# A third seven-product pair for the keys and values of a cross-attention

## The chip, the cores and the metric

The kernel runs on one core of a Trainium2 chip. The metric is the time of one execution on the device in microseconds (us), the median of three runs. Engines are called by the profile's names: PE is TensorE's matmul, PEld its weight load, DVE VectorE, ACT ScalarE, POOL GpSimd, SP the engine that issues the loads.

## What is computed

One encoder layer on x (256 frames x 2048) with 256 memory tokens, all float32: a half-step SwiGLU, a mixer of pooling and gated linear attention, cross-attention on the memory, a second half-step SwiGLU, a last norm. The change touches the keys and values of the cross-attention alone:

```python
def mem_cross_attention(h, mem_h, w_q, w_kv, w_o):
    q = (h @ w_q).reshape(b, s, XATTN_HEADS, XATTN_HEAD_DIM)             # 4 heads of 512
    kv = (mem_h @ w_kv).reshape(b, mem_h.shape[1], 2, XATTN_HEADS, XATTN_HEAD_DIM)
    k, v = kv[:, :, 0], kv[:, :, 1]
    logits = jnp.einsum('bshd,bmhd->bhsm', q, k).astype(jnp.float32) * (XATTN_HEAD_DIM ** -0.5)
    p = jax.nn.softmax(logits, axis=-1).astype(v.dtype)
    o = jnp.einsum('bhsm,bmhd->bshd', p, v).reshape(b, s, D_MODEL)
    return o @ w_o
```

So `mem_h @ w_kv` is a product of 256 x 2048 by 2048 x 4096.

## The kernel before

**Float32 as two halves.** Each float32 operand is split into a high part (a rounded copy, made by ScalarE) and a low part (the rest, a subtraction on VectorE), and a product of two operands is three matmuls: high by high, high by low, low by high. Activations lie transposed in `xs` and `ys`, by 16 k-tiles of 128, high and low; the 256 rows are two halves of 128. A weight tile `raw` is split into `wh` and `wl`.

**Blocks and units.** `block_s` computes 1024 output columns (two groups of 512, j = 0 and 1). It walks over the 2048 inner elements in eight units, each a pair g of k-tiles: one transfer of 1 MB from the weights, a split, then products on TensorE. Keys and values take four blocks, in this order: first key block (heads 0 and 1), first value block, second key block, second value block.

**Plain units.** In a plain unit (`unit_p`) each of 2 banks x 2 halves x 2 k-tiles takes 3 matmuls of 128 x 512: 24. Its split is one `wh` (ScalarE, 128 x 2048, line 1579) and one `wl` (VectorE, line 453).

**Sevens.** A pair with its 2 k-tiles, 2 halves and 2 groups of columns is a 2 x 2 by 2 x 2 product of blocks, and can be had with seven block products in place of eight, from sums of blocks. Such a unit (`unit_s`, `seven`) takes 7 x 3 = 21 matmuls (line 507). Its split (`split_seven`) makes four sums of weight blocks, T (three VectorE additions, line 486), splits three blocks of `raw` themselves into `xh` and `xl` (lines 279, 280; products P1, P3 and P2 read them) and T into `wh` and `wl` (lines 489, 453; P5, P7, P6 and P4 read them). Sums of activation blocks are made once for each pair by `Sums.make` (lines 424 to 436 on VectorE, then two splits, lines 285 and 286); they lie in a tile `ye`, and one of them takes the place of a part of `xs`, so that a pair whose sums are made is a seven from then on. `Sums("ye", xs, (0, 4), True, 2)` names the pairs 0 and 4, and room for two in one tile. The parts of the first seven of a block open two further bank pairs; after the last seven `combine` adds the parts (lines 574 to 579), and after the last unit `join` adds them to the whole (line 589).

**Buffers.** `raw`, `wh` and `wl` have three buffers each. T, `xh` and `xl` have homes that change with the stage. In the feed-forward stages each tag has its own; during keys and values these hold, so that `xh` and `xl` both come from the two buffers called "att":

```python
    KV_HOMES = {"T": [("sg", D, 2)], "xh": [("att", 3 * NB, 2)], "xl": [("att", 3 * NB, 2)]}
```

**Order.** `Stream` emits units in sequence, with the splits two units ahead of the products. `st.op(f, n)` puts other work n units later: `turn_K` transposes and splits keys, `logits` and `probs` make the softmax, `values` multiplies with it, `mem_fold` turns the memory into `xs`. `among_weights` and `in_turn` keep VectorE's and ScalarE's work in the order of emission among the splits; beyond that a planner of the framework sets the order of each engine's instructions when the kernel is built, and on the chip each engine runs its own in that order. Part of a `wl` next to a `combine` or `join` goes to GpSimd (line 457). Loads are issued by SP, one for each unit, when a `raw` buffer is free.

The eight pairs of a block come in the order `KV_ORDER = (1, 5, 2, 0, 3, 6, 4, 7)` in all four blocks: pair 0 is a seven in fourth place, pair 4 in seventh. The sums of pair 0 are made at the start of the first key block, those of pair 4 after its second unit.

Of the kernel before, what the change touches and what calls it, by code (L numbers as in the profile page):

```python
# [20 lines left out]
NB = 512  # L21
# [78 lines left out]
def build(ctx, tc, I, out):  # L100
# [89 lines left out]
    xs = main.tile([P, KT, 2, S], F32R, tag="xs", name="xs")  # L190
# [79 lines left out]
    def among_weights(f):  # L270


        scalar, vector = behind_weights(f)
        latest["vector"] = vector
        if scalar is not None:
            latest["scalar"] = scalar
# [349 lines left out]
    def wload(dst, w, k0, n, n0, cols=NB):  # L626
        nc.sync.dma_start(
            dst, w[k0 * P : (k0 + n) * P, n0 : n0 + cols].rearrange("(k p) n -> p k n", p=P)
        )
# [9 lines left out]
    def wwide(w, n0, k0=0, nk=KT):  # L639

        def src(k):
            def load(raw):
                raw = raw.rearrange("p (k n) -> p k n", n=2 * NB)
                if len(loaded) < 3:
                    for kk in range(2):
                        parts = (0, NB) if not loaded else (0,)
                        for c in parts:
                            n = 2 * NB // len(parts)
                            wload(raw[:, kk : kk + 1, c : c + n], w, k + kk, 1, n0 + c, n)
                else:  # L650
                    wload(raw, w, k, 2, n0, 2 * NB)
                next(first_loads, None)
                loaded.append(1)
            return load
        return [src(k0 + k) for k in range(0, nk, 2)]
# [577 lines left out]
    def homes(of):  # L1233
        return lambda: scope.update(shared={tag: list(of[tag]) for tag in of})
# [47 lines left out]
    w_q, w_kv, w_o = I["xattn_w_q"][0], I["xattn_w_kv"][0], I["xattn_w_o"][0]  # L1282
# [2 lines left out]
    q_sums, Q_ORDER = Sums("ye", xs, (4, 5), True, 2), ((0, 1, 2, 3, 6, 4, 5, 7),  # L1285
                                                        (0, 1, 4, 2, 5, 3, 6, 7))
    Q_SEVENS = ((4,), (4, 5))
    kv_sums, KV_ORDER = Sums("ye", xs, (0, 4), True, 2), (1, 5, 2, 0, 3, 6, 4, 7)
    held = {}

    def ev_Q(b):
# [10 lines left out]
    def turn_K(h):  # L1302
        v = rows_turned(held["K", h])
        K = xa["K", h] = xt("K", [P, 4, 2, M], F32R, tag="kv", bufs=2)
        split(K[:, :, 0, :], K[:, :, 1, :], v)

    def ev_V(b):
        def evict(j, c):
            V = xa["V", 2 * b + j] = xt("V", [P, 2, 2, XHD], F32R, tag="kv", bufs=2)
            split(V[:, :, 0, :], V[:, :, 1, :], c)  # L1310
        return evict

    def logits(h):
        ps = ptile(uid("pl"))
        for t in range(2):
            tok = slice(t * P, (t + 1) * P)
            parts = [(d, a, b) for d in range(4) for a, b in ((0, 0), (0, 1), (1, 0))]
            for i, (d, a, b) in enumerate(parts):
                nc.tensor.matmul(  # L1319
                    ps[:, t, :M], ys[:, 4 * h + d, a, tok], xa["K", h][:, d, b, :],  # L1320
                    start=i == 0, stop=i == 11,
                )
        scale = XHD ** -0.5
        nm, sm = xt("nm", [P, 2], bufs=2), xt("sm", [P, 2], bufs=2)
        nc.vector.tensor_reduce(out=nm, in_=ps[:, :, :M], axis=AX.X, op=ALU.max)
        nc.vector.tensor_scalar_mul(nm, nm, -scale)
        pr = xa["P", h] = xt("P", [P, 2, M], bufs=2)
        for t in range(2):
            nc.scalar.activation(
                pr[:, t, :], ps[:, t, :M], AF.Exp, scale=scale, bias=nm[:, t : t + 1],  # L1330
                accum_out=sm[:, t : t + 1],
            )
        nc.vector.reciprocal(out=sm, in_=sm)
        for t in range(2):
            nc.vector.tensor_scalar_mul(pr[:, t, :], pr[:, t, :], sm[:, t : t + 1])

    def probs(h):
        ps = ptile(uid("pt"))
        for mtile in range(2):
            for t in range(2):  # L1340
                nc.tensor.transpose(
                    ps[:, mtile, t * P : (t + 1) * P], xa["P", h][:, t, mtile * P : (mtile + 1) * P], ident
                )
        if h % 2 == 0:
            xt("PT", [P, D], F32R)
        PT = xa["PT", h] = xa["PT"][:, h % 2 * 4 * S : (h % 2 + 1) * 4 * S].rearrange(
            "p (m a s) -> p m a s", m=2, a=2
        )
        split(PT[:, :, 0, :], PT[:, :, 1, :], ps[:, :, :S])

    def values(h):
        for p in range(2):
            ps = ptile(uid("pv"))
            for d in range(2):
                col = slice((2 * p + d) * P, (2 * p + d + 1) * P)
                parts = [(m, a, b) for m in range(2) for a, b in ((0, 0), (0, 1), (1, 0))]
                for i, (m, a, b) in enumerate(parts):
                    nc.tensor.matmul(  # L1358
                        ps[:, d, :S], xa["V", h][:, m, a, col], xa["PT", h][:, m, b, :],
                        start=i == 0, stop=i == 5,  # L1360
                    )
            split_pair(ys, 4 * h + 2 * p, ps[:, :, :S])
# [8 lines left out]
            for c, after in enumerate((5, 7, 6, 9)):  # L1371
                st.op(lambda c=c: mem_fold(c), after)
    st.op(homes(KV_HOMES))
    for g, after in zip(kv_sums.pairs, (0, 2)):
        st.op(lambda g=g: among_weights(lambda: kv_sums.make(g)), after)
    for b in range(2):
        block_s(wwide(w_kv, b * 2 * NB), xs, kv_sums, KV_ORDER, lambda j, c, b=b: held.__setitem__(
            ("K", 2 * b + j), c))
        for j in (1, 0):
            h = 2 * b + j  # L1380
            st.op(lambda h=h: turn_K(h), 1)
        for h in (2 * b, 2 * b + 1):
            st.op(lambda h=h: logits(h), 2)
            st.op(lambda h=h: probs(h), 3)
        block_s(wwide(w_kv, D + b * 2 * NB), xs, kv_sums, KV_ORDER, ev_V(b))
        for h in (2 * b, 2 * b + 1):
            st.op(lambda h=h: values(h), 1)
# [211 lines left out]
def program(shapes):  # L1599
    import concourse.bacc as _bacc  # L1600

    nc = _bacc.Bacc("TRN2", target_bir_lowering=False, num_devices=1)
    args = {
        name: nc.dram_tensor(f"in_{name}", shapes[name], F32, kind="ExternalInput").ap()
        for name in _INS
    }
    out = nc.dram_tensor("out", _OUT, F32, kind="ExternalOutput").ap()
    with tile.TileContext(nc, schedule_with_timeline_sim=True) as tc, ExitStack() as ctx:
        build(ctx, tc, args, out)
    return nc  # L1610
# [10 lines left out]
```

## Time and profile before

| | |
|---|---|
| median of three runs | 2083.23 us (2082.67 to 2083.72) |
| the profiled execution | 2082.87 us |
| its span, first to last instruction | 2081.1 us |
| mean granted TensorE clock | 0.999 |
| PE busy | 2069.6 us (99%) |
| DVE busy | 1786.6 us (86%) |
| ACT busy | 1138.7 us (55%) |
| DMA, mean | 209 GB/s |

Times in the profile are those of one execution. A busy time of PE counts pipelined matmuls with modelled ends, so the pace of TensorE is read from starts: a run of n matmuls in the chain and its length. The name of a tile tells its kind: L507 products are those of sevens, L362 those of plain units. In a row of groups the last column is the idle time of the engine just before such instructions and what ended it. The four blocks of keys and values lie between 1090 and 1290 us.

### The profile page before, as it was taken

What the parts mean: (1) busy time and instruction counts of PE and PEld (TensorE: products, weight loads), DVE (VectorE), ACT (ScalarE), POOL (GpSimd) and SP (SyncE); (2) the same over time, 40 slices, a digit from 0 to 9 for tenths busy, and PEclk for the clock granted to TensorE, in tenths of its full rate; (3) what the DMA queues carried; (4) which work ended last, traced back from release to release, by engine and by line L of the source; (5) the groups of instructions that cost most, each with busy time, mean ns of one, the idle gap of its engine ahead of it and who ended that gap; (6) DMA issues with size and microseconds to landing.
All of it is one profiled execution on the core that took longest, in us unless ns stands there. A gap on an engine that the chain in (4) does not pass through costs nothing.

```text
span 2081.1 us, 24343 instructions
## 1 busy us (share of the span) xinstructions
PE 2069.6 (99%) x9660; PEld 1727.6 (83%) x9660; DVE 1786.6 (86%) x1670; ACT 1138.7 (55%) x1128; POOL 98.4 (5%) x87
## 2 busy tenths in 40 slices
PE   9999999999999999999999999999999999999998
PEld 7888888888888888888888888888888888888886
DVE  7998899989998677679788777879988999889987
ACT  7655455644654545455755444656554555545554
POOL 0000000000000000000000000000100010000001
PEclk9999999999999999999999999999999999999999
DMA  7666666566656755557655455666576665676664
GB/s 264 207 201 227 235 223 219 185 223 239 227 199 218 249 167 182 162 185 272 226 179 190 162 182 180 205 222 203 181 242 212 237 207 193 223 242 222 210 226 151
DMA packets 131178, 435.95 MB, mean 209 GB/s; under 512 B 9844, under 2 KB 13528, under 8 KB 130680
## 3 DMA queue, kind: packets, MB, share of 16 engines
q1 hardware_dynamic: 130888, 433.86, 61.9%
q8 instruction: 76, 1.25, 0.2%
q10 hardware_dynamic: 176, 0.53, 0.1%
q14 instruction: 38, 0.31, 0.0%
HBM read 417.58 MB, written 16.78 MB: 209 GB/s over the span
## 4 chain that ended last, share of the span: by engine, by line
PE 99%; DMA 0%; DVE 0%; ACT 0%; SPq 0%; DVEq 0%; issue 0%; ACTq 0%
PE pt L362 59%; PE pt L507 27%; PE pa L347 7%; PE pb L362 2%; PE ph L780 1%; PE pl L1319 1%; PE pv L1358 1%; PE px L791 1%; PE pp L1012 0%; PE pe L362 0%; DMA x<-in_x 0%; PE pa L1039 0%; PE po L1161 0%; PE tm L1267 0%; PE px L717 0%; PE pq L1148 0%
## 5 line engine op out<-in xcount | busy, mean ns | idle before, releaser
L362 PE MATMUL pt<-wh,xs 128*128 128x512 f32 x2128 | 682.4, 390 | 0.1
L453 DVE TENSOR_TENSOR wl<-raw,wh 128x2048 fp32r<-128x2048 f32 (+1 forms) x256 | 552.1, 2162 | 141.7 <-ACT wh L1579 141.3
L1579 ACT CAST wh<-raw 128x2048 fp32r<-128x2048 f32 x256 | 489.4, 1913 | 300.7 <-PE pt L362 134.5
L362 PEld LDWEIGHTS pt<-wh,xs 128*128 128x128 f32 x2128 | 398.7, 188 | 81.9 <-ACT xs L236 0.4
L362 PE MATMUL pt<-wh,ys 128*128 128x512 f32 x1472 | 463.9, 389 | 0.0
L489 ACT CAST wh<-T 128x1024 fp32r<-128x1024 f32 x236 | 248.1, 1055 | 366.7 <-DVE T L486 355.8
L362 PE MATMUL pt<-wl,xs 128*128 128x512 f32 x1064 | 414.5, 390 | 0.0
L362 PEld LDWEIGHTS pt<-wh,ys 128*128 128x128 f32 x1472 | 276.2, 188 | 56.9
L362 PE MATMUL pt<-wl,ys 128*128 128x512 f32 x736 | 286.8, 390 | 0.0
L453 DVE TENSOR_TENSOR wl<-T,wh 128x2048 fp32r<-128x2048 f32 (+1 forms) x118 | 264.7, 2243 | 0.8 <-ACT wh L489 0.4
L362 PEld LDWEIGHTS pt<-wl,xs 128*128 128x128 f32 x1064 | 199.8, 188 | 41.0
L280 DVE TENSOR_TENSOR xl<-raw,xh 128x1536 fp32r<-128x1536 f32 x118 | 206.7, 1751 | 18.9 <-ACT xh L279 18.9
L279 ACT CAST xh<-raw 128x1536 fp32r<-128x1536 f32 x118 | 174.6, 1480 | 44.0 <-PE pt L507 35.1
L486 DVE TENSOR_TENSOR T<-T,raw 128x512 f32<-128x512 f32 x236 | 162.9, 690 | 6.2
L362 PEld LDWEIGHTS pt<-wl,ys 128*128 128x128 f32 x736 | 138.2, 188 | 28.6
L486 DVE TENSOR_TENSOR T<-raw 128x1024 f32<-128x1024 f32 x118 | 143.8, 1218 | 0.5
L507 PE MATMUL pt<-wh,xs 128*128 128x512 f32 x364 | 141.8, 390 | 0.0
L457 POOL TENSOR_TENSOR wl<-raw,wh 128x768 fp32r<-128x768 f32 x40 | 74.1, 1852 | 1376.2 <-DVE wl L453 1339.2
L507 PE MATMUL pt<-xh,xs 128*128 128x512 f32 x364 | 135.8, 389 | 0.0
L347 PE MATMUL pa<-xs,wh 128*128 128x512 f32 x384 | 135.6, 397 | 0.0
L507 PE MATMUL pt<-wh,xe 128*128 128x512 f32 x320 | 124.3, 389 | 0.0
L347 PE MATMUL pa<-xs,wl 128*128 128x256 f32 x384 | 106.8, 282 | 0.0
(248 smaller groups left out, 2312.4 us busy)
## 6 DMA issues: line engine op xcount, KB each, us to landing
raw<-in_ffn_w_down SPq DMA_DIRECT2D x88, 1024.0 KB, 5.6
raw<-in_ffn_w_up SPq DMA_DIRECT2D x80, 1024.0 KB, 5.0
raw<-in_ffn_w_gate SPq DMA_DIRECT2D x77, 1024.0 KB, 5.1
raw<-in_w_in SPq DMA_DIRECT2D x32, 1024.0 KB, 5.3
raw<-in_xattn_w_kv SPq DMA_DIRECT2D x32, 1024.0 KB, 5.0
raw<-in_w_out SPq DMA_DIRECT2D x16, 1024.0 KB, 5.6
raw<-in_xattn_w_q SPq DMA_DIRECT2D x16, 1024.0 KB, 5.6
raw<-in_xattn_w_o SPq DMA_DIRECT2D x16, 1024.0 KB, 5.6
```

What stands on the lines that cost most here:

```text
L279: in_turn("scalar", lambda: nc.scalar.copy(hi, src))
L280: in_turn("vector", lambda: nc.vector.tensor_tensor(out=lo, in0=src, in1=f32(hi), op=ALU.subtract))
L347: nc.tensor.matmul(o, w, x, start=k == 0 and i == 0, stop=last and i == 1)
L362: nc.tensor.matmul(ps, a, w, start=first and i == 0, stop=last and i == 2)
L453: in_turn("vector", lambda: nc.vector.tensor_tensor(out=lo[:, :n], in0=src[:, :n], in1=f32(hi[:, :n]), op=ALU.subtract))
L457: rest = nc.gpsimd.tensor_tensor(out=lo[:, n:], in0=src[:, n:], in1=f32(hi[:, n:]), op=ALU.subtract)
L486: in_turn("vector", lambda: nc.vector.tensor_tensor(out=o, in0=a, in1=b, op=ALU.add))
L489: in_turn("scalar", lambda: nc.scalar.copy(th[:, c], t[:, c]))
L507: nc.tensor.matmul(banks[n], x, w, start=n in fresh and j == 0, stop=n in ends and j == 2)
L780: nc.tensor.transpose(v[:, i, h * P : (h + 1) * P], g[:, h, i * P : (i + 1) * P], ident)
L791: nc.tensor.transpose(v[:, j, h * P : (h + 1) * P], x[:, h, j * P : (j + 1) * P], ident)
L1579: in_turn("scalar", lambda: nc.scalar.copy(hi, raw))
```

## The change

Pair 2 becomes a seven in all four blocks as well. The sums of the three pairs share a tile with room for three. The order of the pairs is (1, 5, 3, 6, 0, 4, 2, 7) in the first key block, so that its sevens stand in fifth, sixth and seventh place, and (1, 5, 3, 0, 6, 4, 2, 7) in the other three, with sevens fourth, sixth and seventh. The sums are made later: pair 0's after the first unit of the first key block, pair 4's after the third, pair 2's after the fourth.

```diff
-    kv_sums, KV_ORDER = Sums("ye", xs, (0, 4), True, 2), (1, 5, 2, 0, 3, 6, 4, 7)
+    kv_sums = Sums("ye", xs, (0, 4, 2), True, 3)
+    KEY_ORDER, KV_ORDER = (1, 5, 3, 6, 0, 4, 2, 7), (1, 5, 3, 0, 6, 4, 2, 7)
...
-    for g, after in zip(kv_sums.pairs, (0, 2)):
+    for g, after in zip(kv_sums.pairs, (1, 3, 4)):
         st.op(lambda g=g: among_weights(lambda: kv_sums.make(g)), after)
     for b in range(2):
-        block_s(wwide(w_kv, b * 2 * NB), xs, kv_sums, KV_ORDER, lambda j, c, b=b: held.__setitem__(
-            ("K", 2 * b + j), c))
+        block_s(wwide(w_kv, b * 2 * NB), xs, kv_sums, KV_ORDER if b else KEY_ORDER,
+                lambda j, c, b=b: held.__setitem__(("K", 2 * b + j), c))
```

The value blocks keep their line, with the new `KV_ORDER`.

## The prediction

> **What bounds the kernel now.** I read the page first (shares of the engines, the chain), then a table of stretches over the four key and value blocks, then the groups with shapes kept apart, then the timeline around single sevens. Of the page:
>
> ```profile
> span 2081.1 us, 24343 instructions
> ...
> PE 2069.6 (99%) x9660; PEld 1727.6 (83%) x9660; DVE 1786.6 (86%) x1670; ACT 1138.7 (55%) x1128; POOL 98.4 (5%) x87
> ...
> PE 99%; DMA 0%; DVE 0%; ACT 0%; SPq 0%; DVEq 0%; issue 0%; ACTq 0%
> ```
>
> TensorE is never idle for long, and the chain that ends last is its own. So a product taken away is time gained, as long as its operands come in time; and the only way in which this change can cost is that they don't. The stretches below are the first key block, the first value block, the second key block and the second value block:
>
> ```profile
> core 0: us, PE busy (x) PEld busy (x) DVE busy (x) ACT busy (x) POOL busy (x), PEclk, DMA share, GB/s
> ...
> 1090.00:1142.00 52.00, 52.00 (x252) 43.61 (x250) 45.59 (x51) 30.59 (x31) 3.70 (x2) 1.00 0.57 190
> 1142.00:1191.00 49.00, 49.00 (x245) 41.49 (x244) 34.63 (x33) 25.14 (x27) 3.72 (x2) 1.00 0.48 162
> 1191.00:1239.00 48.00, 48.00 (x236) 40.63 (x235) 34.30 (x28) 20.99 (x17) 3.71 (x2) 1.00 0.53 176
> 1239.00:1290.00 51.00, 51.00 (x261) 43.47 (x260) 36.90 (x42) 24.49 (x28) 3.71 (x2) 1.00 0.55 185
> ```
>
> TensorE is busy throughout all four, at full clock. VectorE has 6.4 us left in the first and some 14 in each other, DMA is used by half: on the mean there is room for more vector work. The mean does not tell where in a block the room lies, so I go on to single instructions.
>
> **What the change takes away.** A plain pair of k-tiles costs 2 banks x 2 halves x 2 k-tiles x 3 = 24 products, a seven 7 x 3 = 21. The changed kernel has one seven more in each of four blocks: 12 products less, which the built order of its TensorE confirms. What one costs is its spacing in an undisturbed stretch of the chain (start, length, what):
>
> ```profile
> 1383.93 37.64 PE pt L362 x166
> ```
>
> 37.64/166 = 0.227 us. So the gain is 12 x 0.227 = **2.7 us**, all of it on the path. The Trainium skill ("TensorE: Matmul & The Clock Gate", section "Back-to-back issue gap") gives about 0.131 us for a sustained product of 512 columns; by that the gain would be 1.6 us. No stretch here is near it, so the row stands.
>
> **What it adds.** Per seven that was a plain pair: sums of weight blocks (T, L486, three additions), the split of three blocks (xh on ScalarE, xl on VectorE), the split of T (wh, wl), in place of one plain wh and wl. And one more making of activation sums (L424 to L436, two L286). The groups, with mean ns in the last column but one:
>
> ```profile
> L453 DVE TENSOR_TENSOR wl<-raw,wh 128x2048 fp32r<-128x2048 f32 x216 | 493.3, 2287 | 117.3 <-ACT wh L1579 116.9
> L1579 ACT CAST wh<-raw 128x2048 fp32r<-128x2048 f32 x256 | 489.4, 1913 | 300.7 <-PE pt L362 134.5 <-issue 56.4 <-PE pa L347 37.0
> ...
> L489 ACT CAST wh<-T 128x1024 fp32r<-128x1024 f32 x236 | 248.1, 1055 | 366.7 <-DVE T L486 355.8 <-PE pt L507 5.8 <-PE pt L362 4.7
> ...
> L453 DVE TENSOR_TENSOR wl<-T,wh 128x2048 fp32r<-128x2048 f32 x112 | 255.8, 2284 | 0.8 <-ACT wh L489 0.4
> L280 DVE TENSOR_TENSOR xl<-raw,xh 128x1536 fp32r<-128x1536 f32 x118 | 206.7, 1751 | 18.9 <-ACT xh L279 18.9
> ...
> L279 ACT CAST xh<-raw 128x1536 fp32r<-128x1536 f32 x118 | 174.6, 1480 | 44.0 <-PE pt L507 35.1 <-DMA raw<-in_ffn_w_gate 7.0 <-DMA raw<-in_w_out 0.4
> L486 DVE TENSOR_TENSOR T<-T,raw 128x512 f32<-128x512 f32 x236 | 162.9, 690 | 6.2
> L486 DVE TENSOR_TENSOR T<-raw 128x1024 f32<-128x1024 f32 x118 | 143.8, 1218 | 0.5
> ...
> L507 PE MATMUL pt<-wh,xe 128*128 128x512 f32 x320 | 124.3, 389 | 0.0
> ...
> L286 DVE TENSOR_TENSOR ye<-j,ye 128x384 fp32r<-128x384 f32 x17 | 9.4, 551 | 0.0
> ...
> L424 DVE TENSOR_TENSOR j<-xs 128x512 f32<-128x512 f32 x12 | 8.2, 682 | 0.0
> ...
> L436 DVE TENSOR_TENSOR j<-j 128x128 f32<-128x128 f32 x26 | 7.6, 291 | 0.8
> ...
> L286 DVE TENSOR_TENSOR xs<-j,xs 128x128 fp32r<-128x128 f32 x12 | 4.1, 345 | 1.4 <-ACT xs L285 1.2
> ```
>
> A seven takes VectorE 1.22 + 2 x 0.69 + 1.75 + 2.28 = 6.63 us, against 2.29 for a plain pair and against 21 x 0.227 = 4.77 us of its own on TensorE. One making takes 0.68 + 4 x 0.29 + 0.35 + 0.55 = 2.74 us. Over the four blocks that is 4 x 4.34 + 2.74 = 20.1 us more, against some 48 us free: by the mean it fits. But a seven is slower on VectorE than on TensorE, so two sevens in a row need a lead, and the row of L279 shows what prevents one: ScalarE's xh copy waited 35.1 us in sum for TensorE's products of sevens. While the homes for keys and values hold, xh and xl both take the two buffers "att"; one seven fills both, and the next one's xh and xl begin only when TensorE has read the last of them. Here is such a release in the first value block, with what follows it on ScalarE and VectorE (from the timelines of the two engines: start, length, instruction, and in brackets the idle time ahead with what ended it):
>
> ```profile
> 1170.09 1.48 ACT L279 CAST xh<-raw 128x1536 fp32r<-128x1536 f32 x1 [5.79 <-PE pt L507]
> ...
> 1171.61 1.76 DVE L280 TENSOR_TENSOR xl<-raw,xh 128x1536 fp32r<-128x1536 f32 x1 [4.23 <-ACT xh L279]
> 1173.51 2.29 DVE L453 TENSOR_TENSOR wl<-T,wh 128x2048 fp32r<-128x2048 f32 x1
> 1175.72 3.68 DVE L453 TENSOR_TENSOR wl<-raw,wh 128x2048 fp32r<-128x2048 f32 x2
> ```
>
> From release to a finished wl: 1173.51 + 2.29 - 1170.09 = **5.71 us**. The kernel before survives this, because in it a seven in fourth place is followed by two plain pairs (fifth and sixth) and a plain pair needs none of the buffers. The changed order puts sevens sixth and seventh in three blocks, and fifth, sixth and seventh in the first key block. So I count, from the built order, the products that TensorE has in hand over each of these spans.
>
> **The three blocks with sevens fourth, sixth, seventh.** The built order runs the fourth place's first product P1 late, after the plain fifth pair, since its banks come free late (as before); at that release TensorE has 9 products of the fourth place left and 12 of the sixth that don't need its wl: 21 x 0.227 = 4.77. They run out 5.71 - 4.77 = 0.95 us early. From the sixth's wl to the seventh's, VectorE runs T, xl and wl in a row: 6.63 us, less three starts that overlap by 0.08 (1175.80 against 1175.72 above), 6.4. TensorE has 9 products of the sixth, 12 of the seventh and 1 of the eighth: 22 x 0.227 = 4.99. That leaves 1.4. A block: 2.35 us, three blocks: **7.1 us**.
>
> **The first key block.** Its first seven is fifth and reads xh as its 18th of 21 products, so 3 are left, and 12 of the sixth: 15 x 0.227 = 3.40 against 5.71, 2.3 us. From the sixth's wl to the seventh's, VectorE has the third making as well, which the built order puts ahead of the seventh's T: 2.74 + 6.63 - some 0.5 for overlapping starts = 8.9, against 22 products, 4.99: 3.9 us. Together **6.2 us**.
>
> **Restarts.** What a late operand does to TensorE stands in the second query block, where one plain pair between two sevens does not quite cover the same span (release 1063.17, wl done at 1068.92):
>
> ```profile
> 1063.17 1.48 ACT L279 CAST xh<-raw 128x1536 fp32r<-128x1536 f32 x1 [11.12 <-PE pt L507]
> ...
> 1066.49 0.50 PE L507 MATMUL pt<-xl,xs 128*128 128x512 f32 x1
> 1066.63 2.29 DVE L453 TENSOR_TENSOR wl<-T,wh 128x2048 fp32r<-128x2048 f32 x1 [0.19 <-ACT wh L489]
> 1066.83 0.39 PE L507 MATMUL pt<-xh,xs 128*128 128x512 f32 x1
> ...
> 1068.44 0.47 PE L362 MATMUL pt<-wh,xs 128*128 128x512 f32 x1
> ...
> 1068.98 0.50 PE L507 MATMUL pt<-wl,xs 128*128 128x512 f32 x1
> 1069.32 0.39 PE L507 MATMUL pt<-wh,xs 128*128 128x512 f32 x1
> ```
>
> The product with wl comes 0.54 instead of 0.23 us after the one ahead, and the next after it 0.34 instead of 0.23: 0.11 us more for each restart. Restarts ahead of a wait on VectorE are swallowed by that wait; two a block are not: 4 x 0.2 = **0.8 us**.
>
> Behind these waits nothing more is late: after the seventh's wl VectorE has only the eighth's plain 2.29 us while TensorE has 5. ScalarE gains 1.48 + 2 x 1.06 - 1.91 = 1.7 us a seven and is busy half the time. The load queue's order stays, and its transfers are as many. POOL's shares are as many. The larger tile of sums is written where the old one was, and free then.
>
> **The sum.** 7.1 + 6.2 + 0.8 - 2.7 = **+11.4 us**, 0.5%. The profiled execution took 2082.87 us, 1.8 of it around its span of 2081.1, and becomes 2094.3 with a span of 2092.5; it lies 0.4 below the median of 2083.23, against which the time is **2094.6 us**.
>
> **Rivals.**
> - The waits are covered and only the gain is left: 2083.2 - 2.7 = 2080.5. For it: the feed-forward blocks run four sevens in eight, two of them adjacent, with 0.0 idle before their products (L507 with xe above), and these blocks have a quarter of VectorE idle. It would need the next seven's xh and xl to be written before the release, or the 5.71 us to shrink below 4.77 and the row of T, xl, wl below 4.99. Against: there xh and xl have buffers of their own, two each; here one seven fills what there is, and the second query block shows TensorE late even with a plain pair between. Chance 0.06.
> - Only the first key block stalls (its making, its three in a row), and in the others VectorE's work ahead fills in: 2083.2 + 6.2 + 0.2 - 2.7 = 2086.9. Against: their T is queued behind the sixth's wl. Chance 0.07.
> - The delay runs on: the eighth pair and the joins come late in every block by about a microsecond too. 2094.6 + 4 = 2098.6. For it: VectorE's join and combine stand right behind. Chance 0.10.
> - The clock falls in the pauses. In the table every stretch has 1.00, and no pause in it was long. The kernel's first transposes (the timeline) came at half the later pace:
>
> ```profile
> 1.43 2.82 PE L206 MATMUL pwarm<-ident 128*128 128x128 f32 x12 [1.43 <-POOL ident masks.py:199]
> ```
>
> against some in the chain, late:
>
> ```profile
> 1140.42 1.75 PE ph L780 x16
> ```
>
> 2.82/12 = 0.235 against 1.75/16 = 0.109. If after each block's pauses a plain pair ran so, 24 x 0.227 = 5.4 us more a block, 2094.6 + 21.8 = 2116. Against: the largest deficit above, 3.9 us, falls in pieces, since xh, wh, xl and wl arrive one after another with products between. Chance 0.04. The Trainium skill ("TensorE: Matmul & The Clock Gate", section "HAM oscillation — how this bites in real kernels") has this as a rule: pauses of more than about 3.4 us put the clock back to half. By its figure that deficit would be enough in one piece; no run here shows it.
> - That the change doesn't do what it says is excluded by the built order: 12 products less, one making and four sevens more.
>
> **How the numbers follow.** My forecast, waits of the size worked out, has 0.73. About 0.2% (4.2 us) is what a measurement of this kernel tells from no change, so "same" runs from 2079.1 to 2087.4. The first rival lies in it, and about half of the second's cases. Faster has no case of its own: 0.01. Same 0.11, slower 0.88. The range: the overlap of starts, and what VectorE gets done ahead, can take a third off the 13.3 us of waits (4.4: 2090.2, rounded to 2090); the third rival ends it above, 2098.6, rounded to 2099. Left out are the first two rivals, the clock and some of the third.
>
> **What would show it.** In the profile after: TensorE's products of sevens (L507) get idle time of some 13 us, ended by VectorE's xl and wl and ScalarE's xh, where now there is next to none, six of it between the fifth and seventh place of the first key block and some 2.4 in each other block; the products with xs and ye number 12 less in sum; VectorE's idle ahead of L280 stays, ended by ScalarE. It is wrong if TensorE shows no such waits in the four stretches, if they stand in front of plain pairs, if the first key block's aren't two to three times each other's, or if the clock falls.

## The result, and the profile after

| | before | after |
|---|---|---|
| median | 2083.23 us (2082.67 to 2083.72, 6 runs) | 2096.60 us (2096.37 to 2097.39, 6 runs) |
| span of the profiled execution | 2081.1 us | 2094.7 us |
| mean granted TensorE clock | 0.999 | 0.997 |

The changed kernel takes 1.0064 times as long, with a 95% interval of 1.0052 to 1.0075: 13.4 us more, where 11.4 were forecast. The page of the changed kernel:

```profile
span 2094.7 us, 24351 instructions
...
PE 2075.2 (99%) x9648; PEld 1726.8 (82%) x9648; DVE 1804.3 (86%) x1693; ACT 1146.1 (55%) x1138; POOL 98.5 (5%) x87
...
PE 97%; DVE 2%; ACT 1%; issue 0%; DVEq 0%; POOL 0%; ACTq 0%; POOLq 0%
```

TensorE has its 12 products less (9648 against 9660), and is nonetheless counted busy for 5.6 us longer: late products and those at a slower clock have longer records (0.50 and 0.63 us below, 0.80 for one that is both, against 0.39). The chain of before was TensorE's alone; now VectorE has 2% and ScalarE 1% of it. Who waited for whom on TensorE (in total, times, longest):

```profile
PE pt L507 <- DVE xl L280: 5.8, 8, 1.9
...
PE pt L507 <- DVE wl L453: 1.3, 4, 0.3
PE pt L507 <- ACT wh L489: 1.2, 1, 1.2
PE pt L507 <- ACT xh L279: 0.7, 1, 0.7
```

Before, no row of L507 stood in this view. Now every wait of note is a seven's, for its own split: 9.0 us of idle time in sum. In the first value block the timelines of ScalarE and VectorE show the two spans that the prediction counted:

```profile
1175.70 1.48 ACT L279 CAST xh<-raw 128x1536 fp32r<-128x1536 f32 x1 [3.30 <-PE pt L507]
...
1177.21 1.76 DVE L280 TENSOR_TENSOR xl<-raw,xh 128x1536 fp32r<-128x1536 f32 x1 [4.09 <-ACT xh L279]
1179.11 2.29 DVE L453 TENSOR_TENSOR wl<-T,wh 128x2048 fp32r<-128x2048 f32 x1
1181.32 1.22 DVE L486 TENSOR_TENSOR T<-raw 128x1024 f32<-128x1024 f32 x1
...
1185.57 2.28 DVE L453 TENSOR_TENSOR wl<-T,wh 128x2048 fp32r<-128x2048 f32 x1
```

From release to the sixth's wl: 1179.11 + 2.29 - 1175.70 = 5.70 us (5.71 was taken). From there to the seventh's: 1185.57 + 2.28 - 1181.40 = 6.45 (6.4). VectorE sat idle for 4.09 us ahead of it all: room that it has on the mean and cannot use, since the buffers are not free. And the first key block, on TensorE's timeline, from the last product of its first seven on:

```profile
1118.51 0.39 PE L507 MATMUL pt<-wh,xs 128*128 128x512 f32 x1
1119.56 0.73 PE L507 MATMUL pt<-xh,xs 128*128 128x512 f32 x2 [0.66 <-ACT xh L279]
...
1121.36 0.50 PE L507 MATMUL pt<-xl,xs 128*128 128x512 f32 x1 [0.35 <-DVE xl L280]
...
1126.44 0.50 PE L507 MATMUL pt<-xh,ye 128*128 128x512 f32 x1
1128.11 0.51 PE L507 MATMUL pt<-wh,xs 128*128 128x512 f32 x1 [1.16 <-ACT wh L489]
1130.50 0.80 PE L507 MATMUL pt<-xl,xs 128*128 128x512 f32 x1 [1.89 <-DVE xl L280]
1131.09 0.63 PE L507 MATMUL pt<-xh,xs 128*128 128x512 f32 x1
1131.52 0.63 PE L507 MATMUL pt<-xl,xs 128*128 128x512 f32 x1
...
1136.79 0.40 PE L507 MATMUL pt<-wh,ye 128*128 128x512 f32 x1
```

Between 1126.44 and 1130.50 a single product starts. After that they start 0.43 us apart (1131.09, 1131.52), not 0.227. The stretches give the reason (length, busy times of PE, PEld, VectorE, ScalarE and GpSimd, then the granted clock ahead of the DMA share; the last three rows meet where the granted clock changes or, at 1126.23, 3.41 us before it falls):

```profile
1118.00:1130.00 12.00, 8.12 (x29) 4.86 (x28) 10.14 (x13) 7.90 (x9) 0.00 (x0) 0.98 0.28 89
1126.23:1129.64 3.41, 1.22 (x4) 0.37 (x2) 3.38 (x5) 2.04 (x3) 0.00 (x0) 1.00 0.00 0
1129.64:1136.46 6.82, 5.96 (x14) 4.71 (x15) 6.61 (x4) 3.83 (x3) 0.07 (x1) 0.50 0.56 164
1136.46:1139.88 3.42, 3.42 (x16) 2.81 (x16) 1.96 (x3) 2.40 (x2) 1.78 (x1) 1.00 0.92 311
```

From 1129.64 on, for 6.8 us, TensorE's clock was granted at half. From 1118.51 to 1136.79 lie 41 starts: 18.28 - 41 x 0.227 = 9.0 us lost in the first key block. The same count over the sevens of the other three blocks gives 2.6 us each, 7.7 in all. Together 9.0 + 7.7 - 2.7 = 14.0, against 13.6 between the spans; TensorE's wait for x at the very start, 0.8 us before and none after, is the one other difference in its waits.

### The profile page after: what moved, and what is told of

The parts are those of the page before. It is cut to its first block, busy times and chain, and to the rows that moved or that the text cites. A ratio compares the mean times of both kernels' runs of the same rounds, so it can differ in the third digit from the quotient of the medians.

```text
span 2094.7 us, 24351 instructions
## 1 busy us (share of the span) xinstructions
PE 2075.2 (99%) x9648; PEld 1726.8 (82%) x9648; DVE 1804.3 (86%) x1693; ACT 1146.1 (55%) x1138; POOL 98.5 (5%) x87
## 4 chain that ended last, share of the span: by engine, by line
PE 97%; DVE 2%; ACT 1%; issue 0%; DVEq 0%; POOL 0%; ACTq 0%; POOLq 0%
PE pt L362 57%; PE pt L507 26%; PE pa L347 6%; PE pb L362 2%; PE ph L780 1%; PE pl L1320 1%; PE pv L1359 1%; DVE wl L453 1%; DVE xl L280 1%; PE px L791 1%; DVE T L486 0%; ACT xh L279 0%; PE pp L1012 0%; PE pe L362 0%; ACT wh L489 0%; PE px L717 0%
## 5 line engine op out<-in xcount | busy, mean ns | idle before, releaser
L362 PE MATMUL pt<-wh,xs 128*128 128x512 f32 x2064 | 663.0, 391 | 0.0
L453 DVE TENSOR_TENSOR wl<-raw,wh 128x2048 fp32r<-128x2048 f32 (+1 forms) x252 | 542.7, 2159 | 129.7 <-ACT wh L1580 129.1
L1580 ACT CAST wh<-raw 128x2048 fp32r<-128x2048 f32 x252 | 481.3, 1913 | 290.2 <-PE pt L362 119.5
L489 ACT CAST wh<-T 128x1024 fp32r<-128x1024 f32 x244 | 256.3, 1054 | 367.3 <-DVE T L486 356.5
L362 PEld LDWEIGHTS pt<-wh,xs 128*128 128x128 f32 x2064 | 387.1, 188 | 79.5 <-ACT wh L1580 0.2
L362 PE MATMUL pt<-wl,xs 128*128 128x512 f32 x1032 | 402.1, 390 | 0.0
L453 DVE TENSOR_TENSOR wl<-T,wh 128x2048 fp32r<-128x2048 f32 (+1 forms) x122 | 273.8, 2244 | 0.9 <-ACT wh L489 0.4
L280 DVE TENSOR_TENSOR xl<-raw,xh 128x1536 fp32r<-128x1536 f32 x122 | 213.6, 1751 | 21.3 <-ACT xh L279 21.3
L362 PEld LDWEIGHTS pt<-wl,xs 128*128 128x128 f32 x1032 | 193.9, 188 | 39.4
L507 PE MATMUL pt<-wh,xs 128*128 128x512 f32 x380 | 148.6, 391 | 1.2 <-ACT wh L489 1.2
L507 PE MATMUL pt<-xh,xs 128*128 128x512 f32 x380 | 142.0, 391 | 0.7 <-ACT xh L279 0.7
L507 PE MATMUL pt<-wh,xe 128*128 128x512 f32 x320 | 124.3, 389 | 0.0
```

The costliest lines, as they stand in the source:

```text
L280: in_turn("vector", lambda: nc.vector.tensor_tensor(out=lo, in0=src, in1=f32(hi), op=ALU.subtract))
L362: nc.tensor.matmul(ps, a, w, start=first and i == 0, stop=last and i == 2)
L453: in_turn("vector", lambda: nc.vector.tensor_tensor(out=lo[:, :n], in0=src[:, :n], in1=f32(hi[:, :n]), op=ALU.subtract))
L489: in_turn("scalar", lambda: nc.scalar.copy(th[:, c], t[:, c]))
L507: nc.tensor.matmul(banks[n], x, w, start=n in fresh and j == 0, stop=n in ends and j == 2)
L1580: in_turn("scalar", lambda: nc.scalar.copy(hi, raw))
```

## The experiments

The unchanged kernel, measured beside them, took 2083.1 to 2083.2 us.

**Buffers of their own for xh.**

```diff
-    KV_HOMES = {"T": [("sg", D, 2)], "xh": [("att", 3 * NB, 2)], "xl": [("att", 3 * NB, 2)]}
+    KV_HOMES = {"T": [("sg", D, 2)], "xh": [("kv", D, 2)], "xl": [("att", 3 * NB, 2)]}
```

> The changed kernel with one edit: during keys and values xh takes the two buffers of the key and value tiles ("kv") and xl alone the two of "att", so that two sevens can be split at a time; orders, sums and products are untouched. Theory (the waits come from the shared pair of buffers): the 2.4 us of waits in each of the last three blocks all but go (0 to 0.5 us left a block), in the first key block VectorE's row of three sevens and two makings, 3 x 6.63 + 2 x 2.74 = 25.4 us, stands against 14.3 us of products and the 10.9 us of the two plain pairs ahead, so 0 to 2.5 us of its 8.9 us remain, and the clock doesn't fall: 2083.2 - 2.7 + (0 to 4) = 2081 to 2084.5, most likely 2082.5. Rival (VectorE is simply too slow for three sevens, whatever the buffers): the waits stay, 2094 to 2097. Rival (the tile's own release, keys and values, becomes the wait): 2085 to 2090, with ScalarE's xh waiting for products of logits or values.

Measured: 2084.12 us (11 runs), 1.0003 of the kernel before (0.9994 to 1.0011). With the same products, sums and orders, one line takes away 12.5 of the 13.4 us. TensorE's waits:

```profile
PE px L717 <- DMA x<-in_x: 1.5, 1, 1.5
PE pwarm L206 <- POOL ident masks.py:199: 1.4, 1, 1.4
PE pt L507 <- DVE xl L280: 1.4, 1, 1.4
PE pt L507 <- DVE PT L286: 0.5, 1, 0.5
```

Of the sevens' splits one wait is left, in the first key block, where VectorE does three sevens and two makings in a row; the 0.5 is a bank that the softmax frees late. That some wait would stay there was foreseen; the time lies 1.6 us above the value called likeliest, within the range. In the profiled execution the load of x at the very start has a part in it (0.7 us more waiting than in that of the kernel before), which the edit doesn't touch. ScalarE's xh copies now wait for products of the logits, 17.3 us in two waits, as the second rival had it, but TensorE does not wait for them in turn, and the time that this rival names, 2085 to 2090, does not come. The rival that three sevens in eight are too much for VectorE falls: it does the same work here in 2082.4 us of span.

**The first key block undone.** In the changed kernel:

```diff
-    KEY_ORDER, KV_ORDER = (1, 5, 3, 6, 0, 4, 2, 7), (1, 5, 3, 0, 6, 4, 2, 7)
+    KEY_ORDER, KV_ORDER = (1, 5, 2, 0, 3, 6, 4, 7), (1, 5, 3, 0, 6, 4, 2, 7)
...
-    for g, after in zip(kv_sums.pairs, (1, 3, 4)):
+    for g, after in zip(kv_sums.pairs, (0, 2, 8)):
...
         block_s(wwide(w_kv, b * 2 * NB), xs, kv_sums, KV_ORDER if b else KEY_ORDER,
+                sevens=(0, 4, 2)[: 2 + b], evict=
                 lambda j, c, b=b: held.__setitem__(("K", 2 * b + j), c))
```

> The changed kernel, but the first key block as in the kernel before (pairs 0 and 4 as sevens in fourth and seventh place, pair 2 plain, 24 products); the sums of pair 2 are made after that block, and the other three blocks have three sevens each. 9 products less than before in place of 12. Theory (each block's waits are its own): 2083.2 - 9 x 0.227 + 3 x 2.46 = 2088.6, with the clock at full speed throughout since no pause is longer than 1.4 us. Rival (part of the later blocks' waits is handed on by the first): 2083 to 2086. Rival (the third making, wherever it is, costs): 2091 or more, with a new wait where it now stands.

Measured: 2088.94 us (9 runs), 1.0027 (1.0017 to 1.0037). The waits of the other blocks are their own: nothing is handed on by the first, and each costs what it cost in the changed kernel (2.5 to 2.6 us by starts).

**The making earlier.**

```diff
-    for g, after in zip(kv_sums.pairs, (1, 3, 4)):
+    for g, after in zip(kv_sums.pairs, (1, 2, 3)):
```

> The changed kernel with the sums of pairs 4 and 2 made one unit earlier each (after the first, second and third unit of the first key block in place of first, third and fourth). Theory (the making between the sixth's wl and the seventh's T stretches that wait, and the long pause lets the clock fall): the making falls into the time in which VectorE waits for the release anyway (4.2 us idle before the sixth's xl), the span from wl to wl shrinks from 8.9 to 6.4 us, the wait by 2.5; the longest pause is then some 1.5 us, the clock stays at full speed, another 2.5: 2096.6 - 5.0 = 2091.6. If the clock falls for another reason than the pause: 2094.1, with a stretch at 0.50 in the first key block. If the making's place doesn't matter: 2096.6.

Measured: 2091.98 us (4 runs), 1.0040 (1.0026 to 1.0054). The first key block of this kernel, and in it the stretch with its longest wait (1.84 us start to start):

```profile
1090.00:1145.00 55.00, 52.49 (x247) 42.72 (x245) 52.21 (x62) 32.67 (x35) 3.73 (x2) 1.00 0.55 179
1119.00:1125.00 6.00, 4.49 (x19) 3.06 (x18) 5.97 (x6) 3.25 (x4) 0.00 (x0) 1.00 0.36 117
```

The clock stays at 1.00. So 4.6 us came from where VectorE's 2.7 us of making stood: in the way of a split that TensorE waited for, or ahead of it, in a time when VectorE was idle anyway. Two parts are in this, the shorter wait and the clock that did not fall. By starts this block loses 3.6 us, 5.4 less than in the changed kernel (the spans differ by 5.1); the half clock had cost 2.8 of them there, as worked out below, and the rest is the wait.

**Two sevens, but adjacent.** The kernel before, with nothing added:

```diff
-    kv_sums, KV_ORDER = Sums("ye", xs, (0, 4), True, 2), (1, 5, 2, 0, 3, 6, 4, 7)
+    kv_sums = Sums("ye", xs, (0, 4), True, 2)
+    KEY_ORDER, KV_ORDER = (1, 5, 2, 0, 3, 6, 4, 7), (1, 5, 2, 3, 6, 0, 4, 7)
...
-        block_s(wwide(w_kv, b * 2 * NB), xs, kv_sums, KV_ORDER, lambda j, c, b=b: held.__setitem__(
-            ("K", 2 * b + j), c))
+        block_s(wwide(w_kv, b * 2 * NB), xs, kv_sums, KV_ORDER if b else KEY_ORDER,
+                lambda j, c, b=b: held.__setitem__(("K", 2 * b + j), c))
```

> The kernel before, with its two pairs 0 and 4 as sevens and as many products, but with pair 0 moved from fourth to sixth place in the last three blocks (order 1, 5, 2, 3, 6, 0, 4, 7), so that the two sevens stand next to each other; the first key block is as before. Theory (adjacency with one pair of buffers costs, not the third seven's work): from release to wl 5.71 us against 3 + 12 products, 3.40: 2.3 us a block and 0.1 for the restart, three blocks: 2083.2 + 7.2 = 2090.4. Rival (the amount of vector work is what costs): 2083.2, no waits.

Measured: 2089.80 us (6 runs), 1.0031 (1.0020 to 1.0042): 6.6 us for a change of order alone, without one product or one addition more. TensorE's waits for sevens come three times each, once in each block whose order changed:

```profile
PE pt L507 <- ACT xh L279: 2.0, 3, 0.7
...
PE pt L507 <- DVE xl L280: 1.0, 3, 0.4
```

**The first key block in the others' order.**

```diff
-    KEY_ORDER, KV_ORDER = (1, 5, 3, 6, 0, 4, 2, 7), (1, 5, 3, 0, 6, 4, 2, 7)
+    KEY_ORDER, KV_ORDER = (1, 5, 3, 0, 6, 4, 2, 7), (1, 5, 3, 0, 6, 4, 2, 7)
...
-    for g, after in zip(kv_sums.pairs, (1, 3, 4)):
+    for g, after in zip(kv_sums.pairs, (0, 2, 3)):
```

> The changed kernel with the first key block in the order of the others (sevens fourth, sixth, seventh; makings before the first unit, after the second and after the third), buffers shared as in the changed kernel. Theory (a wait of 2.46 us for each fourth-sixth-seventh block, and the first key block pays for its three in a row): all four blocks alike, 2083.2 - 2.7 + 4 x 2.46 = 2090.3, clock at full speed. In the first block no product of softmax or values holds up the fourth place's banks, so its release can come earlier and its wait be less, down to 1.5 us: 2089.3. Rival (the first key block's wait is that of a block with three makings, in any order): 2093 or more.

Measured: 2090.41 us (5 runs), 1.0035 (1.0021 to 1.0048). By starts, the first block now loses 2.1 us and the others 2.6 each, as in the changed kernel. So 6.2 us of the time after (2096.60 - 2090.41) were due to the first key block's three sevens in a row with a making between, and to what they did to the clock.

**Sevens spread.**

```diff
-    KEY_ORDER, KV_ORDER = (1, 5, 3, 6, 0, 4, 2, 7), (1, 5, 3, 0, 6, 4, 2, 7)
+    KEY_ORDER, KV_ORDER = (1, 5, 0, 3, 4, 6, 2, 7), (1, 5, 0, 3, 4, 6, 2, 7)
...
-    for g, after in zip(kv_sums.pairs, (1, 3, 4)):
+    for g, after in zip(kv_sums.pairs, (0, 1, 3)):
```

> The changed kernel with sevens third, fifth and seventh in all four blocks (order 1, 5, 0, 3, 4, 6, 2, 7; makings before the first unit, after the first and after the third), buffers shared. Theory: a plain pair between two sevens gives TensorE 24 more products, 5.4 us, in which the split can be done; the second query block, spaced so, lost 0.7 us. Four blocks: 2083.2 - 2.7 + 4 x 0.7 = 2083.3; where the planner puts the plain pair ahead of the seven (late banks) the cover is gone for one of the two spans, up to 1.5 us more a block: up to 2089. Rival (the third seven's vector work costs whatever the spacing): 2090 or more.

Measured: 2088.52 us (9 runs), 1.0027 (1.0017 to 1.0037), at the upper end and 5.2 us above the value named first: the 0.7 us a block taken from the second query block held for the last two blocks (0.9 each) and not for the first two. Their waits are of other kinds:

```profile
PE pt L362 <- DVE wl L453: 2.1, 2, 1.1
...
PE pt L507 <- ACT P L1330: 1.0, 1, 1.0
PE pt L507 <- DVE xl L280: 0.8, 3, 0.3
```

A plain pair's wl comes late behind the makings in the first key block, and a seven's banks behind the softmax in the first value block. Spacing alone is no full remedy; which place of the makings would be was not tried.

**A probe of the clock.** The kernel before, with VectorE's xl written again in the seventh place of each block:

```diff
         split_weights(rh, rl, raw[:, NB:])
+        for _ in range({204: 5, 212: 4, 220: 4, 228: 5}.get(u, 0)):
+            in_turn("vector", lambda: nc.vector.tensor_tensor(
+                out=rl, in0=raw[:, NB:], in1=f32(rh), op=ALU.subtract
+            ))
```

> A probe of the clock: the kernel before, in which VectorE writes the same xl again 5, 4, 4 and 5 times in the seventh place of the first key, first value, second key and second value block, so that TensorE waits once in each, in one piece, by about 3.0, 4.2, 2.4 and 6.0 us. Theory (a pause of some 3 to 4 us, in one piece or nearly, lets the clock fall to half for some 6 us): products 0.43 us apart after the pauses of 4.2 and 6.0, 0.23 after that of 2.4, either after 3.0; about 2083 + 16 of pauses + 2.5 for each fall whose time isn't hidden = 2102 to 2107. Rival (what fell in the changed kernel was due to its several short waits in a row, not to the pause): 0.23 throughout, 2099.

Measured: 2105.07 us in one run. Start to start, the pauses were 3.28, 4.58, 2.77 and 6.37 us. The second shortest and then the shortest, on TensorE's timeline (L511 is the line of the sevens' products in this kernel):

```profile
1125.82 0.39 PE L511 MATMUL pt<-wh,xs 128*128 128x512 f32 x1
1129.10 0.50 PE L511 MATMUL pt<-xl,xs 128*128 128x512 f32 x1 [2.89 <-DVE xl L489]
1129.43 0.40 PE L511 MATMUL pt<-xh,xs 128*128 128x512 f32 x1
...
1234.03 0.39 PE L511 MATMUL pt<-wh,xs 128*128 128x512 f32 x1
1236.79 0.80 PE L511 MATMUL pt<-xl,xs 128*128 128x512 f32 x1 [2.38 <-DVE xl L489]
1237.39 0.63 PE L511 MATMUL pt<-xh,xs 128*128 128x512 f32 x1
1237.81 0.63 PE L511 MATMUL pt<-xl,xs 128*128 128x512 f32 x1
```

After 3.28 us products go on at full pace (0.33 and then 0.23 apart), after 2.77, where full pace was expected, at 0.43; after 4.58 and 6.37 too they slow to 0.43, the former about a microsecond after the restart. So a single pause does it, and its length alone doesn't decide. What does can be read from where the granted clock changes. In this trace it changes at 1185.54, 1188.95, 1236.74, 1240.15, 1291.35 and 1298.18 us: from the first, that is 1, 15, 16, 31 and 33 steps of 3.413 us. In the changed kernel 1129.64 and 1136.46 are two such steps apart. Here are the steps around the pauses of 3.28 and of 2.77 us, in the columns of the stretches above:

```profile
1124.10:1127.51 3.41, 2.11 (x10) 1.41 (x8) 3.34 (x3) 1.91 (x1) 0.00 (x0) 1.00 0.00 0
1127.51:1130.92 3.41, 1.82 (x8) 1.51 (x9) 3.41 (x2) 0.00 (x0) 0.00 (x0) 1.00 0.26 38
1130.92:1134.33 3.41, 3.41 (x16) 2.61 (x15) 3.41 (x3) 0.76 (x2) 0.00 (x0) 1.00 0.68 269
...
1233.33:1236.74 3.41, 1.08 (x5) 0.56 (x3) 3.38 (x3) 1.91 (x1) 0.00 (x0) 1.00 0.00 0
1236.74:1240.15 3.41, 3.36 (x8) 2.68 (x9) 3.41 (x2) 0.00 (x0) 0.00 (x0) 0.50 0.67 191
1240.15:1243.56 3.41, 3.41 (x16) 2.81 (x16) 3.03 (x3) 1.26 (x2) 0.94 (x1) 1.00 0.67 193
```

The longer pause is shared by two steps, in which PE is still busy for 2.11 and 1.82 us, and the clock stays. The shorter one lies nearly whole in one step, with PE busy for 1.08 us, and the next step is at half clock. In the changed kernel the step ahead of the fall had 1.22. In all ten traces of this case the clock falls after every full-speed step in which PE was busy for 1.39 us or less, and after none with 1.60 or more (busy as the profile counts it). The steps lie elsewhere in each trace: counted in steps from the first instruction, the changes are 0.95 past a whole number in the changed kernel's and 0.33 in this one. So whether a pause of some 2 to 4 us (an estimate from these rows) costs the clock depends on where it meets the steps; that the same kernel meets them well in one execution and badly in another was not measured. Pauses of up to 1.84 us (the longest in the kernel with the making earlier) left the clock alone.

**Own buffers, and the third pair in three blocks.** In the changed kernel:

```diff
-    KV_HOMES = {"T": [("sg", D, 2)], "xh": [("att", 3 * NB, 2)], "xl": [("att", 3 * NB, 2)]}
+    KV_HOMES = {"T": [("sg", D, 2)], "xh": [("kv", D, 2)], "xl": [("att", 3 * NB, 2)]}
...
-    KEY_ORDER, KV_ORDER = (1, 5, 3, 6, 0, 4, 2, 7), (1, 5, 3, 0, 6, 4, 2, 7)
+    KEY_ORDER, KV_ORDER = (1, 5, 2, 0, 3, 6, 4, 7), (1, 5, 3, 0, 6, 4, 2, 7)
...
-    for g, after in zip(kv_sums.pairs, (1, 3, 4)):
+    for g, after in zip(kv_sums.pairs, (0, 2, 5)):
...
+                sevens=(0, 4, 2)[: 2 + b], evict=
```

> A version put together from the runs so far: xh in the two buffers of the key and value tiles, the first key block as in the kernel before (two sevens, pair 2 plain, its sums made after the fifth unit), three sevens fourth, sixth and seventh in the other three. 9 products less than before. Theory: with buffers of its own e1 kept waits of 0.8 and 0.4 us in the two value blocks and 1.8 in the first key block; the last goes with the two sevens there: 2083.2 - 2.0 + 1.2 = 2082.4, under both kernels but hardly more than can be measured. Rival (the third making costs where it now stands, in the first key block): 2083.5 to 2085.

Measured: 2082.75 us (11 runs), 0.9998 (0.9989 to 1.0007). It beats the changed kernel by some 13.9 us; against the kernel before no difference can be told.

## Why the prediction was right

**The gain**, 12 products of 0.227 us or 2.7 us, agrees with the sum over the blocks, which closes to within a microsecond; no run has the gain alone.

**The waits of the three later blocks**, 7.1 us and 0.6 of restarts, were 7.7. The step they rest on, that xh and xl of a seven wait for TensorE's last read of the seven before, is shown by the run with buffers of their own (2084.12) and from the other side by the two adjacent sevens of the kernel before (2089.80).

**The first key block**, 6.2 us and 0.2, was 9.0. The spans are as worked out: 1123.73 - 1118.03 = 5.70 and from the sixth's wl to the seventh's 8.91 (8.9 forecast), by these rows of its ScalarE and VectorE:

```profile
1118.03 1.48 ACT L279 CAST xh<-raw 128x1536 fp32r<-128x1536 f32 x1 [5.11 <-PE pt L507]
...
1121.44 2.29 DVE L453 TENSOR_TENSOR wl<-T,wh 128x2048 fp32r<-128x2048 f32 x1
1123.64 0.69 DVE L424 TENSOR_TENSOR j<-xs 128x512 f32<-128x512 f32 x1
...
1130.36 2.28 DVE L453 TENSOR_TENSOR wl<-T,wh 128x2048 fp32r<-128x2048 f32 x1
```

What was left out is the clock. From 1130.50 to 1136.56, 14 products take 6.06 us in place of 3.18; less 0.1 for the restart, that is 2.8 us, and without it the block lost 6.2. That is the term that the sum lacked. It stood among the rivals, at a chance of 0.04, with a plain pair slowed in every block; it came in one block, and there some 13 products long. The reason given against it, that the deficit falls in pieces, was the step that failed: with pieces of 1.67 and 2.39 us and one product between, PE was busy for only 1.22 of the 3.41 us ahead of the fall. By the Trainium skill ("TensorE: Matmul & The Clock Gate", section "HAM oscillation — how this bites in real kernels") pauses of over about 3.4 us set the clock back; the falls here, after no pause above 2.39 us, and in the probe, after one of 2.77, came earlier than that, and the measurement decides.

**The rivals.** That the waits are covered fell, and so did the one in which only the first key block stalls (2088.94 with that block undone). That the delay runs on fell too: the three later blocks lost no more than the waits counted for the sixth and seventh place.

**The signs.** The waits stand where they were named, in the four stretches and ahead of sevens, and are ended by the splits named and, once, by a wh. Their idle time is 9.0 us (4.4 in the first key block, some 1.5 in each other) where some 13 was named, since a late product's longer record hides a part; by starts they are 6.2 and 2.6. One sign went against the forecast by its own words: it was to be wrong if the clock fell. With the clock the first key block lost 3.5 times as much as another (9.0 against 2.6), more than the two to three that were named; without it 2.4 times. So the mechanism of the waits held and the assumption of a full clock did not. That the time stays within 2090 to 2099 is in part luck: the fall came once and cost 2.8 us, and the upper bound had been set by a rival that did not come.

## What to carry to other kernels

Before work is moved to an engine that has room on the mean, look where in the stage the room lies: if it is ahead of a buffer's release, it can't be used, and what counts is the span from release to the finished operand against the work that the bound engine has in hand. Two units of the costly kind in a row had to share one set of buffers here; a second home for one of the two operands, in buffers that another step leaves free in that stage, took back 12.5 of the 13.4 us. A pause of the matmul engine can cost more than its length: look at the granted clock behind it, in slices of a few us.

## What the runs showed of the hardware

After a late operand, at full clock, the next product starts 0.34 instead of 0.227 us on (333 to 341 ns behind the waits of the key and value blocks), so each restart costs 0.11 us of its own. The granted clock changed only on steps of 3.413 us, and fell to half behind each step in which PE was busy for 1.39 us or less, behind none with 1.60 or more. So it fell after pauses of 2.77, 4.58 and 6.37 us, and after 1.67 and 2.39 with one product between, and not after one of 3.28 that two steps shared. In these blocks half clock lasted one or two steps (3.41 or 6.83 us), with products 0.427 us apart, and cost 1.3 to 2.8 us beyond the pause. Where between 1.39 and 1.60 us the bound lies was not tried.
